# Two projections side by side through the tiles of x, and the place of one constants' transfer, in a hybrid decoder trunk

## The chip, the core and the metric

The kernel runs on one core of a Trainium2 chip. The metric is device time in microseconds (us) of one execution; the time of a kernel is the median of its runs. The core has five engines that run side by side, each through its own queue of instructions in order: TensorE (PE in the profile, its weight loads PEld), VectorE (DVE), ScalarE (ACT), GpSimd (POOL) and SyncE (SP, which here only issues transfers). They wait for one another through semaphores.

## The reference

A decoder trunk of two layers over 512 tokens of 1024 channels, in float32. Layer 0 is the one that matters here: its mixer projects the normed x to 1536 columns, of which 512 go to a causal pooling branch (u) and 2 times 512 to a gated causal convolution of width 31 with a LayerNorm and a swish (a and b); both results are concatenated and projected back.

```python
def pool_conv_mixer(h, w_in, pool_w, pool_scale, dw_w, dw_b, ln_g, ln_b, w_out):
    z = h @ w_in
    u, glu_a, glu_b = jnp.split(z, [POOL_W, POOL_W + CONV_W], axis=-1)
    ...
    ya = jnp.einsum("btgc,gcd->btgd", pooled, pool_w).reshape(b, t, POOL_W) * pool_scale
    gl = glu_a * jax.nn.sigmoid(glu_b)
    cv = causal_dwconv(gl, dw_w) + dw_b
    yb = jax.nn.silu(layernorm(cv, ln_g, ln_b))
    return jnp.concatenate([ya, yb], axis=-1) @ w_out

for l in range(DEPTH):
    h = rmsnorm(x, norm_mix_g[l])
    x = x + (pool_conv_mixer(h, ...) if l % 2 == 0 else mla_attention(h, ...))
    x = x + memory_cross_attention(rmsnorm(x, ...), rmsnorm(mem, ...), ...)
    x = x + conv_ffn(rmsnorm(x, norm_ffn_g[l]), ...)
return rmsnorm(x, final_norm_g)
```

## The kernel before

Activations lie with channels on the 128 partitions and the 512 tokens along the free axis, so x is 8 tiles of 128x512. A product of two float32 numbers is made of three passes: each operand is split into a rounded part (`hh`, `wh`: a cast on ACT) and a rest (`hl`, `wl`: a subtraction on DVE), and `mm3` (L177 to 181) multiplies hi by hi, hi by lo and lo by hi. One output tile of a projection over 8 tiles of x is therefore 24 matmuls ("products" below) of 128x512, and each needs a weight block of 128x1024 that SP loads (`load_w`, L169), ACT casts (L173) and DVE subtracts (L174).

The mixer (L871 to L1092) has these stages.

- **Opening** (L878): the first projection, n = 0, takes tile after tile of x as it lands, with the split of x in `Norm.split` (L286 on ACT, L287 on DVE). Its weights come in two halves of 128x512. Behind it the large constants' transfer `con[:, KD:]` (128 rows of 451 numbers) is issued from ACT's queue.
- **Twelve projections** (L1008): `order` is b, a for each of four convolution tiles, then four u. The norm's rate (`row_rate`, from `nat` tiles that ACT squares, L253) is applied afterwards: `finish` (L993) multiplies a projection's PSUM bank by the rate `rb`, which PE spreads over the partitions (L268, after `RB_K` of 8 tiles of the third projection) and ACT copies. `finish` of an a-tile completes a gated tile, `gl`.
- **Taps**: the convolution is 31 multiply-adds on DVE for each of four tiles (L932, L934), less five of the last tile that PE does with diagonal weights `dg` (L938). The 119 DVE taps are handed out in small portions beside other work: `taps(PACE[0])` for each projection from the point at which a `gl` exists, then `PACE[1]` and `PACE[2]` in the steps of the first memory projection (`memory_kv`, 8 steps and 8 steps), then `PACE[3]` in `filler` (L1058). `PACE` is `(3, 3, 2, 3)`.
- **Filler** (L1058 to L1082): the second memory projection (16 steps, each yields 2), then the pooling half of the output projection (8 outputs, each 12 products, two steps of 1 each, L1061 to L1066). When no tap is left, this loop starts the stages of `normalise` (L952), one at a time with the numbers in `LATE` of steps between them: the mean over channels (a matmul on PE, L962), its subtraction and the squares, the sum (transposes on PE, L241), the Newton steps of a reciprocal root on DVE (L222), its spread (L268, `lb`), the scale and the swish. Stages that the loop did not start run behind it (L1084 to L1088).
- **Last**: the convolution half of the output projection (L1090), 8 outputs of 12 products over the four `yb` tiles.

The order that each engine gets is made by a scheduler from the order of the code and from priorities; weight preparation has a priority of 40 instructions ahead (L172). The lines that decide which portion a loop step gets:

```python
for step in filler():
    if left[0]:
        if step == 2 or left[0] % 2:
            taps(PACE[3])
        ...
    if not left[0] and due <= 0 and stage < len(LATE):
        next(late, None)
```

Weight blocks rotate through three buffers (`wh`, `wl`), raw blocks through four (`wr`), PSUM through eight banks. `early_parts` (L158) is a second set of two buffers, which the FFN uses.

Of the kernel before, what the change touches and what calls it, by code (L numbers as in the profile page):

```python
# [15 lines left out]
ALU = mybir.AluOpType  # L16
# [3 lines left out]
P = 128  # L20
# [3 lines left out]
KD = D // P  # L24
# [33 lines left out]
PE_PACE = 2  # L58
PACE = (3, 3, 2, 3)
MEM1_AT = 10  # L60
RB_K = 6
LATE = (1, 4, 1, 3, 1, 4, 1)
FFN_GROUPS = (4, 4, 4, 4, 6)
PLAIN_PAIRS = 5
# [41 lines left out]
def kernel(ctx: ExitStack, tc: tile.TileContext, a):  # L106
    nc = tc.nc
    vec, act, pe, pool, sp = nc.vector, nc.scalar, nc.tensor, nc.gpsimd, nc.sync
# [10 lines left out]
    def uid(s):  # L119
        count[0] += 1  # L120
        return f"{s}{count[0]}"
# [4 lines left out]
    def bank(name="ps", shape=(P, T)):  # L126
        return pp.tile(list(shape), F32, tag="ps", name=uid(name))
# [4 lines left out]
    def f(t):  # L132
        return t.bitcast(F32)


    con = cp.tile([P, NCOL], F32, tag="con", name="con")
# [11 lines left out]
    def load_raw(src, n):  # L148
        raw = wp.tile([P, WCOLS], F32, tag="wr", name=uid("wr"), bufs=4)
        sp.dma_start(raw[:, :n], src)  # L150
        return raw

    def parts():
        hi = wp.tile([P, WCOLS], F32R, tag="wh", name=uid("wh"), bufs=3)
        lo = wp.tile([P, WCOLS], F32R, tag="wl", name=uid("wl"), bufs=3)
        return hi, lo

    def early_parts():  # L158

        hi = wp.tile([P, WCOLS], F32R, tag="wh1", name=uid("wh1"), bufs=2)  # L160
        lo = wp.tile([P, WCOLS], F32R, tag="wl1", name=uid("wl1"), bufs=2)
        return hi, lo

    def low_by_dma(lo, raw, src):

        act.mul(lo, raw, -1.0)  # L166
        pool.dma_start(lo, src, accum_op=ALU.add)  # L167

    def load_w(src, n):  # L169
        raw = load_raw(src, n)  # L170
        hi, lo = parts()
        with tc.high_priority(offset=AHEAD):  # L172
            act.copy(hi[:, :n], raw[:, :n])  # L173
            vec.tensor_tensor(lo[:, :n], raw[:, :n], f(hi[:, :n]), ALU.subtract)  # L174
        return hi, lo

    def mm3(ps, ah, al, bh, bl, first, last, more=False):  # L177

        pe.matmul(ps, ah, bh, start=first, stop=False, skip_group_check=more)  # L179
        pe.matmul(ps, ah, bl, start=False, stop=False, skip_group_check=more)  # L180
        pe.matmul(ps, al, bh, start=False, stop=last, skip_group_check=more)  # L181

    class Linear:
# [6 lines left out]
        def load(self, k):  # L190
            c = k // KD
            if c not in self.w:
                n = min(KD, self.nk - c * KD) * P
                self.w[c] = load_w(self.src[:, c * KD * P:c * KD * P + n], n)
            return self.w[c]
# [9 lines left out]
    def linear(src, xs):  # L205
        return Linear(src, len(xs)).run(xs, 0, len(xs))
# [664 lines left out]
    def mixer(norm, nxt):  # L871
# [3 lines left out]
        def project(i):  # L875
            return linear(a["pc_in"][i], norm.h)

        def opening(i):  # L878

            ps = bank("lin")  # L880
            half = KD // 2
            for k in range(KD):
                if k % half == 0:
                    hi, lo = load_w(a["pc_in"][i][:, k * P:(k + half) * P], half * P)
                sp.dma_start(x[k], a["xT"][:, k, :])
                norm.split(k)
                c = slice(k % half * P, (k % half + 1) * P)
                mm3(ps, hi[:, c], lo[:, c], *norm.h[k], k == 0, k == KD - 1)
            return ps

        def window(i, t):
# [95 lines left out]
        def taps(n):  # L987
            for _ in range(min(n, left[0])):
                next(conv)

        sig, us, parts = {}, [], []
# [13 lines left out]
        order = [(k, i) for i in range(CT) for k in "ba"] + [("u", i) for i in range(CT)]  # L1005
        base = {"b": 2 * CT, "a": CT, "u": 0}
        wait = []
        for n, (kind, i) in enumerate(order):  # L1008
            if n == 2:
                lin.run(norm.h, 0, RB_K)  # L1010
                rb = norm.wide()
                wait.append((kind, i, lin.run(norm.h, RB_K, KD)))
            else:
                wait.append((kind, i, (project if n else opening)(base[kind] + i)))
            if n == 0:
                act.dma_start(con[:, KD:], a["con"][:, KD:])
            if n == 1:
                lin = Linear(a["pc_in"][base[order[2][0]] + order[2][1]], KD)
                lin.load(0)
                norm.r = row_rate(a["xN"], TB, "rx")  # L1020
            elif n > 1:
                if n == MEM_AT[0]:
                    mem.rate()
                if n == MEM_AT[1]:
                    mem.scale()
                if n == MEM_AT[2]:
                    scaled = [], []
                    for _ in memory_gain(0, mem.raw, *scaled):
                        pass
                while len(wait) > 1:  # L1030
                    finish(*wait.pop(0))
                if gl:
                    taps(PACE[0])
# [417 lines left out]
```

## Time and profile before

| What | Value |
|---|---|
| median of 3 runs | 1383.91 us (1382.83 to 1383.95) |
| the profiled execution, its own time | 1383.12 us |
| its span in the trace | 1381.3 us |
| PE busy | 1352.6 us (98%) |
| DVE busy | 1020.0 us (74%) |
| ACT busy | 748.8 us (54%) |
| the chain that ended last | PE 88%, DVE 8%, ACT 2%, issue 1% of the span |

The time of a run is 1.8 us more than its span: work ahead of and behind the first and the last instruction. In the rows below, "start us, duration us, engine, line, operation, output<-inputs, shape, count" stand in this order, and what ended an idle stretch is in brackets at the end. Matmuls overlap, so the distance from one start to the next says how long a product holds PE, and its duration does not.

### The profile page before, as it was taken

How to read it: one execution, taken by the hardware profiler on the slowest of the kernel's cores; microseconds unless marked ns; L12 is line 12 of the kernel's file. 1: busy time of each engine (PE TensorE's matmuls, PEld its weight loads, DVE VectorE, ACT ScalarE, POOL GpSimd, SP SyncE). 2: the span in 40 equal slices, each digit the busy share in tenths (PEclk: the TensorE clock that was granted, in tenths of full speed). 3: DMA queues.
4: the chain of work that ended last, by engine and by line, in shares of the span. 5: the costliest groups of instructions: out<-in, count | busy, mean ns of one | idle time of the engine just before them, and what ended most of it. 6: DMA issues, size and time to landing. Idle time of an engine off the chain costs nothing.

```text
span 1381.3 us, 20270 instructions
## 1 busy us (share of the span) xinstructions
PE 1352.6 (98%) x7756; PEld 1168.1 (85%) x7756; DVE 1020.0 (74%) x1897; ACT 748.8 (54%) x1264; POOL 52.9 (4%) x71
## 2 busy tenths in 40 slices
PE   8999999999989999999999999999999999999997
PEld 6888978888879999999887776888887899999987
DVE  6999989554787777776869775755549777777765
ACT  6416456445655555554447786644556555555433
POOL 0000000001100000000000000000011000000000
PEclk9999999999999999999999999999999999999999
DMA  9335634118835545553321113321486455555421
GB/s 327 99 104 188 217 104 151 61 38 207 184 91 130 159 124 138 134 137 94 106 81 50 43 47 107 107 77 61 124 188 124 130 132 143 134 136 144 111 73 62
DMA packets 57265, 168.01 MB, mean 122 GB/s; under 512 B 6480, under 2 KB 8144, under 8 KB 57168
## 3 DMA queue, kind: packets, MB, share of 16 engines
q1 hardware_dynamic: 47664, 135.55, 30.6%
q0 software_dynamic: 7776, 28.32, 12.3%
q10 hardware_dynamic: 1728, 2.86, 0.6%
q8 instruction: 60, 0.98, 0.3%
q14 instruction: 37, 0.30, 0.1%
HBM read 162.50 MB, written 4.19 MB: 121 GB/s over the span
## 4 chain that ended last, share of the span: by engine, by line
PE 88%; DVE 8%; ACT 2%; issue 1%; DMA 0%; SPq 0%; DVEq 0%; ACTq 0%
PE lin L179 11%; PE lin L181 11%; PE lin L180 11%; PE xyz L179 8%; PE xyz L180 8%; PE xyz L181 8%; PE down L180 4%; PE down L179 4%; PE down L181 4%; DVE cv L934 3%; PE s L1273 1%; PE mpv L1310 1%; DVE wl L174 1%; PE t L1298 1%; PE vx L180 1%
## 5 line engine op out<-in xcount | busy, mean ns | idle before, releaser
L179 PE MATMUL xyz<-th,wh 128*128 128x256 f32 x816 | 230.8, 284 | 10.6 <-ACT q L737 10.6
L181 PE MATMUL xyz<-th,wl 128*128 128x256 f32 x816 | 231.5, 284 | 0.0
L180 PE MATMUL xyz<-tl,wh 128*128 128x256 f32 x816 | 231.3, 284 | 0.0
L173 ACT CAST wh<-wr 128x1024 fp32r<-128x1024 f32 (+3 forms) x120 | 112.7, 944 | 161.8 <-issue 60.6
L179 PE MATMUL lin<-hh,wh 128*128 128x512 f32 x432 | 171.0, 396 | 5.9 <-ACT hh L286 5.9
L179 PEld LDWEIGHTS xyz<-th,wh 128*128 128x128 f32 x816 | 155.7, 192 | 23.2 <-ACT q L737 14.9
L180 PE MATMUL lin<-hl,wh 128*128 128x512 f32 x432 | 169.7, 393 | 0.0
L181 PE MATMUL lin<-hh,wl 128*128 128x512 f32 x432 | 169.2, 392 | 0.2 <-DVE wl L174 0.2
L180 PEld LDWEIGHTS xyz<-tl,wh 128*128 128x128 f32 x816 | 156.8, 192 | 7.1
L174 DVE TENSOR_TENSOR wl<-wr,wh 128x1024 fp32r<-128x1024 f32 (+3 forms) x120 | 130.1, 1086 | 42.4 <-ACT wh L173 40.9
L181 PEld LDWEIGHTS xyz<-th,wl 128*128 128x128 f32 x816 | 156.7, 192 | 0.0
L565 DVE TENSOR_TENSOR wl<-ws,wh 128x1024 fp32r<-128x1024 f32 x68 | 83.3, 1225 | 61.4 <-ACT wh L564 47.9
L564 ACT CAST wh<-ws 128x1024 fp32r<-128x1024 f32 x68 | 71.3, 1049 | 103.9 <-PE xyz L180 101.3
L179 PE MATMUL down<-fh,dwh 128*128 128x512 f32 x256 | 101.9, 398 | 1.2 <-ACT dwh L218 1.2
L180 PE MATMUL down<-fl,dwh 128*128 128x512 f32 x256 | 102.0, 398 | 0.0
L181 PE MATMUL down<-fh,dwl 128*128 128x512 f32 x256 | 100.5, 393 | 0.5 <-DVE dwl L219 0.5
L179 PEld LDWEIGHTS lin<-hh,wh 128*128 128x128 f32 x432 | 81.6, 189 | 22.3 <-ACT hh L286 6.2
L180 PEld LDWEIGHTS lin<-hl,wh 128*128 128x128 f32 x432 | 81.5, 189 | 18.5 <-DVE hl L287 2.7
L181 PEld LDWEIGHTS lin<-hh,wl 128*128 128x128 f32 x432 | 81.5, 189 | 17.5 <-DVE wl L174 0.6
L167 POOL DMA_DIRECT2D wl<-in_ffn_up x54 | 46.9, 868 | 1058.2 <-ACT wl L166 1058.2
L934 DVE SCALAR_TENSOR_TENSOR cv<-a,con,cv 128x509 f32<-128x509 f32 (+25 forms) x115 | 79.4, 726 | 0.1
L670 ACT ACTIVATE c<-c 128x512 f32<-128x512 f32 x44 | 27.8, 632 | 58.5 <-DVE c L669 58.3
(404 smaller groups left out, 3152.1 us busy)
## 6 DMA issues: line engine op xcount, KB each, us to landing
wr<-in_ffn_up SPq DMA_DIRECT2D x88, 512.0 KB, 4.1
wl<-in_ffn_up POOLq DMA_DIRECT2D x54, 512.0 KB, 5.7
dr<-in_ffn_down SPq DMA_DIRECT2D x64, 256.0 KB, 4.2
wr<-in_xa_wk SPq DMA_DIRECT2D x16, 512.0 KB, 3.5
wr<-in_xa_wv SPq DMA_DIRECT2D x16, 512.0 KB, 4.3
wr<-in_xa_wq SPq DMA_DIRECT2D x16, 512.0 KB, 3.5
wr<-in_xa_wo SPq DMA_DIRECT2D x16, 512.0 KB, 3.5
wr<-in_ffn_down SPq DMA_DIRECT2D x16, 384.0 KB, 3.3
```

The costliest lines, as they stand in the source:

```text
L167: pool.dma_start(lo, src, accum_op=ALU.add)
L173: act.copy(hi[:, :n], raw[:, :n])
L174: vec.tensor_tensor(lo[:, :n], raw[:, :n], f(hi[:, :n]), ALU.subtract)
L179: pe.matmul(ps, ah, bh, start=first, stop=False, skip_group_check=more)
L180: pe.matmul(ps, ah, bl, start=False, stop=False, skip_group_check=more)
L181: pe.matmul(ps, al, bh, start=False, stop=last, skip_group_check=more)
L564: act.copy(hi[:, :n], raw)
L565: vec.tensor_tensor(lo[:, :n], raw, f(hi[:, :n]), ALU.subtract)
L670: act.activation(c, c, AF.Silu)
L934: vec.scalar_tensor_tensor(cv[i][:, s:], gl[i][:, :T - s], w, cv[i][:, s:], ALU.mult, ALU.add)
L1273: pe.matmul(ps[i], q[:, i * P:(i + 1) * P], k[:, :P * (i + 1)], start=True, stop=True)
L1298: pe.transpose(banks[b][:, c:c + P], prob[n][i][:, j * P:(j + 1) * P], ident)
```

## The change

Four things change. The opening now takes two output tiles: b0 and a0 go through the tiles of x together, each with its weights in two halves of 128x512; the second one's split weights lie in the `early_parts` buffers. The large constants' transfer moves from behind the first projection to behind the last split of x, and is held at that place in program order. `RB_K` goes from 6 to 2 and now counts in the fourth projection (n = 3), so `rb` is made there, and `finish` first runs at n = 3 with three projections at once where it ran at n = 2 with two. The third projection is a plain one.

```diff
-RB_K = 6
+RB_K = 2
...
+    pieces = parts, early_parts
...
-        def opening(i):
-
-            ps = bank("lin")
+        def opening(tiles):
+
+            ps = [bank("lin") for _ in tiles]
             half = KD // 2
+            w = {}
+
+            def load(n, k):
+                raw = load_raw(a["pc_in"][tiles[n]][:, k * P:(k + half) * P], half * P)
+                hi, lo = pieces[n]()
+                act.copy(hi[:, :half * P], raw[:, :half * P])
+                vec.tensor_tensor(lo[:, :half * P], raw[:, :half * P], f(hi[:, :half * P]), ALU.subtract)
+                w[n] = hi, lo
+
+            def product(n, k):
+                c = slice(k % half * P, (k % half + 1) * P)
+                mm3(ps[n], w[n][0][:, c], w[n][1][:, c], *norm.h[k], k == 0, k == KD - 1)
+
             for k in range(KD):
                 if k % half == 0:
-                    hi, lo = load_w(a["pc_in"][i][:, k * P:(k + half) * P], half * P)
+                    load(0, k)
                 sp.dma_start(x[k], a["xT"][:, k, :])
                 norm.split(k)
-                c = slice(k % half * P, (k % half + 1) * P)
-                mm3(ps, hi[:, c], lo[:, c], *norm.h[k], k == 0, k == KD - 1)
+                if k % half == 0:
+                    load(1, k)
+                product(0, k)
+                if k % half:
+                    if k % half == 1:
+                        product(1, k - 1)
+                    product(1, k)
+            tc.keep_in_program_order(act.dma_start(con[:, KD:], a["con"][:, KD:]))
             return ps
...
         for n, (kind, i) in enumerate(order):
-            if n == 2:
+            if n == 0:
+                opened = opening([base[kind] + i for kind, i in order[:2]])
+            if n < 2:
+                wait.append((kind, i, opened[n]))
+            elif n == 2:
+                wait.append((kind, i, lin.run(norm.h, 0, KD)))
+            elif n == 3:
+                lin = Linear(a["pc_in"][base[kind] + i], KD)
                 lin.run(norm.h, 0, RB_K)
                 rb = norm.wide()
                 wait.append((kind, i, lin.run(norm.h, RB_K, KD)))
             else:
-                wait.append((kind, i, (project if n else opening)(base[kind] + i)))
-            if n == 0:
-                act.dma_start(con[:, KD:], a["con"][:, KD:])
+                wait.append((kind, i, project(base[kind] + i)))
...
-                while len(wait) > 1:
+                while len(wait) > 1 and n > 2:
                     finish(*wait.pop(0))
                 if gl:
                     taps(PACE[0])
```

Line numbers behind the opening grow by 2 to 26 in the changed kernel. The order that the engines get differs in three places of the mixer.

**ACT, the end of the opening.** `hh` are the splits of x, `wh` weight casts, `dg` the diagonals for PE's taps (they read the large constants), `nat` the squares for the norm's rate. Before:

```order
L944 ACTIVATE dg_736<-ident,con 128x128
L286 ACTIVATE hh_138<-x_77,con 128x512
L944 ACTIVATE dg_739<-ident,con 128x128
L286 ACTIVATE hh_146<-x_78,con 128x512
L944 ACTIVATE dg_769<-ident,con 128x128
L286 ACTIVATE hh_154<-x_79,con 128x512
L944 ACTIVATE dg_772<-ident,con 128x128
L286 ACTIVATE hh_162<-x_80,con 128x512
L173 CAST wh_173<-wr_171 128x1024
```

The same place in the changed kernel:

```order
L288 ACTIVATE hh_196<-x_80,con 128x512
L909 DMA con<-in_con 128x451
L175 CAST wh_210<-wr_208 128x1024
L965 ACTIVATE dg_739<-ident,con 128x128
L175 CAST wh_285<-wr_283 128x1024
L255 ACTIVATE nat_215,rxp_214<-nat_215 128x512
L255 ACTIVATE nat_218,rxp_214<-nat_218 128x512
L965 ACTIVATE dg_742<-ident,con 128x128
L255 ACTIVATE nat_221,rxp_214<-nat_221 128x512
```

The four diagonals moved from between the splits of x to between the weight casts and the squares, behind the transfer of the constants, which ACT now issues after the last split.

**DVE, where the first projections are finished.** `wl_410` and `wl_447` (before) are the weights of n = 5 and n = 6, `wl_413` and `wl_450` in the changed kernel; `b` and `a` are finished tiles, `cv` the taps. Before:

```order
L234 SCALAR_TENSOR_TENSOR rxy_237<-rxt_239,rxy_237 128x4
L174 TENSOR_TENSOR wl_410<-wr_407,wh_409 128x1024
L995 TENSOR_TENSOR b_283<-lin_92,rb_275 128x512
L995 TENSOR_TENSOR a_286<-lin_170,rb_275 128x512
L1000 TENSOR_TENSOR a_286<-a_286,b_283 128x512
L932 TENSOR_SCALAR cv_88<-a_286,con 128x512
L934 SCALAR_TENSOR_TENSOR cv_88<-a_286,con,cv_88 128x511
```

The same place in the changed kernel:

```order
L236 SCALAR_TENSOR_TENSOR rxy_243<-rxt_245,rxy_243 128x4
L176 TENSOR_TENSOR wl_413<-wr_410,wh_412 128x1024
L176 TENSOR_TENSOR wl_450<-wr_447,wh_449 128x1024
L1016 TENSOR_TENSOR b_360<-lin_92,rb_300 128x512
L1016 TENSOR_TENSOR a_363<-lin_93,rb_300 128x512
L1016 TENSOR_TENSOR b_366<-lin_207,rb_300 128x512
L1021 TENSOR_TENSOR a_363<-a_363,b_360 128x512
L1016 TENSOR_TENSOR a_403<-lin_282,rb_300 128x512
L953 TENSOR_SCALAR cv_88<-a_363,con 128x512
```

One more weight block, that of n = 6, now stands ahead of the first finished tile.

**PE, the output projection.** `lin` are outputs of the output projection, their inputs `yah`, `yal` the pooling branch and `ybh`, `ybl` the convolution branch; `mean`, `st` and `rb` are PE's three parts of the convolution's LayerNorm. Before, the mean stands between the first and the second output of the pooling half (`st` and `rb` stand 31 and 50 rows further on, between later outputs):

```order
L179 MATMUL lin_1608<-yah_1019,wh_1611 128x512
L180 MATMUL lin_1608<-yal_1020,wh_1611 128x512
L181 MATMUL lin_1608<-yah_1019,wl_1612 128x512
L962 MATMUL mean_1636<-lacc_1623,om_1627 128x512
L179 MATMUL lin_1638<-yah_928,wh_1641 128x512
L180 MATMUL lin_1638<-yal_929,wh_1641 128x512
```

In the changed kernel the three stand here:

```order
L181 MATMUL lin_1751<-yah_1022,wh_1754 128x512
L182 MATMUL lin_1751<-yal_1023,wh_1754 128x512
L183 MATMUL lin_1751<-yah_1022,wl_1755 128x512
L983 MATMUL mean_1782<-lacc_1776,om_1780 128x512
L243 MATMUL st_1800<-ident,lsq_1784 128x128 x4
L270 MATMUL rb_1824<-ident,lny_1809 128x128 x4
L181 MATMUL lin_1887<-ybh_1839,wh_1890 128x512
L182 MATMUL lin_1887<-ybl_1840,wh_1890 128x512
```

All three moved behind the eighth and last output of the pooling half (`lin_1751`), and follow one another directly, ahead of the first product of the convolution half.

## The prediction

> **What bounds the kernel now.** I read the waits of PE first, since PE is busy 98% of the span: what PE waits for is nearly all that can be won at once.
>
> ```profile
> PE lin L179 <- ACT hh L286: 5.9, 1, 5.9
> PE mean L962 <- DVE lacc L957: 1.5, 1, 1.5
> ```
>
> The columns are the total in us, the times, and the longest. The first is the time to the first product; the second is the only real wait of the mixer, at the mean of its LayerNorm. Next I read PE in order of time in the opening:
>
> ```profile
> 5.85 0.80 PE L179 MATMUL lin<-hh,wh 128*128 128x512 f32 x1 [5.85 <-ACT hh L286]
> ...
> 16.25 0.40 PE L179 MATMUL lin<-hh,wh 128*128 128x512 f32 x1
> ...
> 21.02 0.39 PE L179 MATMUL lin<-hh,wh 128*128 128x512 f32 x1
> ...
> 26.46 0.60 PE L268 MATMUL rb<-ident,rxy 128*128 128x128 f32 x4
> ```
>
> The row at 16.25 is the 4th product of the second projection, the one at 21.02 the first of the third: 21 products in 4.77 us, **0.227 us a product** (24 are 5.44) once all is there. The first two projections, 48 products, took 21.02 - 5.85 = 15.2 us, where 48 at 0.227 are 10.9. So some 4 us are lost in the opening, to the slow first products and to the pace of x.
>
> The end of the mixer, PE first, is the other place that I need:
>
> ```profile
> 177.71 0.39 PE L179 MATMUL lin<-yah,wh 128*128 128x512 f32 x1
> ...
> 182.07 1.10 PE L962 MATMUL mean<-lacc,om 128*128 128x512 f32 x2 [1.47 <-DVE lacc L957]
> ...
> 189.86 0.60 PE L241 MATMUL st<-ident,lsq 128*128 128x128 f32 x4
> ...
> 194.57 0.65 PE L268 MATMUL rb<-ident,lny 128*128 128x128 f32 x4
> ...
> 203.26 0.39 PE L179 MATMUL lin<-ybh,wh 128*128 128x512 f32 x1
> ```
>
> From 177.71 to 203.26 PE does the 96 products of the pooling half, and between them the mean, `st` and `rb`. Between these three, DVE and ACT work for 7 us, 4 us and 8 us, and PE is covered by products all that time. This cover is what the change touches.
>
> **Why the cover goes.** It follows from counting taps, without a time in it. Before, `gl` exists from n = 2, so `PACE[0]` hands out 10 times 3 = 30 taps; the first memory projection 8 times 3 and 8 times 2 = 40; the second 16 times 3 = 48. That leaves 119 - 118 = **1** tap at the first step of the pooling half. One is odd, so `step == 2 or left[0] % 2` holds, the tap is handed out, and `normalise` starts in the loop. In the changed kernel `finish` waits for n = 3, so only 27 are handed out first, and 119 - 27 - 40 - 48 = **4** are left. The steps now yield 1, and 4 is even: none is handed out in 16 steps, `left[0]` never reaches 0, and all stages of `normalise` are emitted behind the loop. The order of the built program agrees: mean, `st` and `rb` stand behind the last pooling product.
>
> **The change part by part.**
>
> *Opening.* PE's clock and the pace of the first products:
>
> ```profile
> 5.85:10.20 4.35, 4.35 (x9) 1.00 1.03 379
> 402.00:406.00 4.00, 4.00 (x17) 0.50 0.30 93
> ```
>
> Nine products started in the first 4.35 us, 0.48 each, though this column grants 1.00 there; the changed kernel has the same x0 first, so I leave these nine as they are. From 10.2 on PE has 39 products left and, with two outputs for each tile of x, always one ready: 39 at 0.227 are 8.9, so the third projection starts at 10.22 + 8.9 + 0.2 for the change of pace = 19.3 instead of 21.02, **1.7 us earlier**. Two more transfers of 256 KB ahead of the last x, and 225 KB of constants fewer, leave the bytes ahead of the last x nearly equal; its last split (12.95 before, see below) may move by a microsecond and still be ahead of PE's need at about 18.
>
> *Constants and rate.* ACT's part of the opening:
>
> ```profile
> 12.95 0.71 ACT L286 ACTIVATE hh<-x,con 128x512 fp32r<-128x512 f32 x1
> ...
> 16.40 0.63 ACT L253 ACTIVATE nat<-nat 128x512 f32<-128x512 f32 x1
> ```
>
> ```profile
> con<-in_con ACTq DMA_DIRECT2D x1, 225.5 KB, 4.0
> ```
>
> ```profile
> 24.94 0.16 DVE L234 SCALAR_TENSOR_TENSOR rxy<-rxt,rxy 128x4 f32<-128x4 f32 x1
> ...
> 28.65 0.68 DVE L995 TENSOR_TENSOR b<-lin,rb 128x512 f32<-128x512 f32 x1
> ```
>
> The first `dg` now waits for the large constants, and queued behind it on ACT are a weight cast and all squares of the rate. Issued at about 12 (12.95 less the four diagonals that are gone) with the 4.0 us to landing of the row above, the constants are there at 16.0; with the diagonal (0.3) and the cast (0.95) the squares start at 17.3, 0.9 late, and three more diagonals between them make 1.8. The rate, 24.94 before, is there at 26.8, `rb` can start at about 27.2. PE would be at `rb` after 31 more products, 19.3 + 7.0 = 26.3. So PE waits 0.9 there, and the lead shrinks from 1.7 to about 0.8. Bounds: no wait (lead 1.7), or the constants 2 us later behind the other transfers (lead -1).
>
> *DVE.* `wl_450` now stands ahead of the first finished tile, and its buffer is free when PE ends n = 3: 27.2 + 0.4 + 17 products = 31.5, plus 2.2 (before, 26.46 to 28.65) is 33.7. DVE starts on taps **5 us later** than at 28.65. What it costs depends on what DVE has to do before each weight block:
>
> ```profile
> 53.41 0.65 DVE cv L934
> 54.06 1.14 DVE wl L174
> ```
>
> At the blocks of the second half of the first memory projection, where PE stands closest behind DVE (below), the changed order has 8 taps and one block fewer ahead: 8 x 0.65 + 1.14 = 6.3 us less work, so the block comes 1.3 us earlier than before. At the third block of the pooling half only the one block is missing, and it comes 5.0 - 1.1 = 3.9 us later, at about 180; PE needs it at 177.71 + 5.4 + 0.2 - 0.8 = 182.5. So I take no new wait on DVE; the margin is 2 us.
>
> ```profile
> 118.12 0.39 PE L179 MATMUL vx<-wh,mh 128*128 128x512 f32 x1
> 118.58 0.50 PE L180 MATMUL vx<-wl,mh 128*128 128x512 f32 x1
> ```
>
> Here PE waited 118.58 - 118.12 - 0.23 = 0.2 us for DVE, which goes. **Lead at the pooling half: 1.0 us**, bounds -1 and 2.
>
> *The end of the mixer.* The pooling half runs through: 177.71 - 1.0 + 96 x 0.227 = 198.5. There PE meets the mean; its input is long there. Then the chain that was covered, with no other work between its links on DVE and ACT:
>
> ```profile
> 21.70 0.17 DVE L256 TENSOR_SCALAR rxq<-rxq 128x4 f32<-128x4 f32 x1
> ...
> 23.69 0.17 DVE L233 TENSOR_TENSOR rxt<-rxt,rxnv 128x4 f32<-128x4 f32 x1
> ```
>
> ```profile
> 183.20 2.48 DVE L966 TENSOR_TENSOR cv<-cv,mean 128x512 f32<-128x512 f32 x4 [0.68 <-PE mean L962]
> 185.60 0.68 DVE L970 TENSOR_TENSOR lsq<-lsq,lq 128x512 f32<-128x512 f32 x1
> ...
> 190.49 0.69 DVE L243 TENSOR_REDUCE ssum<-st 128x4 f32<-128x512 f32 x1 [0.41 <-PE st L241]
> 191.22 0.17 DVE L261 TENSOR_SCALAR lnv<-ssum 128x4 f32<-128x4 f32 x1
> ...
> 195.88 2.50 DVE L977 TENSOR_TENSOR cv<-cv,lb 128x512 f32<-128x512 f32 x4
> ...
> 201.94 0.69 DVE L219 TENSOR_TENSOR ybl<-cv,ybh 128x512 fp32r<-128x512 f32 x1
> ```
>
> ```profile
> 195.26 0.59 ACT L270 COPY lb<-rb 128x512 f32<-128x512 f32 x1 [0.25 <-PE rb L268]
> 195.87 1.28 ACT L978 ACT_TABLE_LOAD   x1
> 197.16 2.94 ACT L978 ACTIVATE cv<-cv,con 128x512 f32<-128x512 f32 x4
> ...
> 200.51 0.62 ACT L218 CAST ybh<-cv 128x512 fp32r<-128x512 f32 x1
> ```
>
> Link by link: mean to its first subtraction 183.20 - 182.07 = 1.1; four subtractions 2.4 and, behind the last of them, the last square 0.6 and the last two sums, 1.3, together 4.3; `st` to the reduction 190.49 - 189.86 = 0.6; the reduction 0.7; the Newton steps as at 21.70 to 23.69 and one more, 2.4; `rb` and the copy 195.26 - 194.57 = 0.7; the copy and the table load 197.16 - 195.26 = 1.9; four swishes 2.9; the cast 0.6. Sum **15.2 us**; with the hops of a few hundredths, and with `st` and `rb` on a slow PE, I take 15.7. In before these links took 201.1 - 182.07 = 19 us, since other work stood between them: that is the other bound of this term.
>
> *PE after the stall.* PE's clock after an idle stretch is shown by the FFN:
>
> ```profile
> 401.69 0.58 PE L179 MATMUL xyz<-th,wh 128*128 128x256 f32 x1 [5.42 <-ACT q L737]
> ...
> 406.76 0.28 PE L181 MATMUL xyz<-th,wl 128*128 128x256 f32 x1
> ```
>
> After 5.4 us of idle the clock is 0.50 (window row above) for about 4.9 us, and products take twice as long. The stall here is three times as long, so the convolution half starts slow: its first 12 products at 0.43, the first two 0.65 apart for the rest of `yb`, take 4.9 us instead of 2.7, 2.2 more. The page "TensorE: Matmul & The Clock Gate" of the Trainium skill, section "What's actually happening", has the half clock after an idle window of about 3.4 us and until a busy window of 3.4 us; the trace agrees on the half clock, but shows 4.9 us of it. With 3.4 us of slow clock the sum would be about 0.7 lower.
>
> *Sum.* The convolution half starts, counted as if at full speed, at 198.5 + 15.7 + 2.2 = 216.4 instead of 203.26: 13.1 us later. What follows it has the same order on PE as before and moves along. Against the profiled execution's own 1383.12 that is **1396.2**; that execution is 0.8 below the median of the runs shown, inside their spread of 1.1.
>
> **The rivals.**
>
> 1. *The stall is there, but cheap.* PE comes back warm (for it: `st` and `rb` touch PE in between; against: the FFN rows) and the lead is whole: 1396.2 - 2.2 - 0.7 = 1393.3. Chance 0.2.
> 2. *The stall is there, and the lead is lost too.* The constants land late, and with them the squares, `rb` and the first tap; the 2 us of margin at the pooling half are used up, and PE waits there as well. For it: DVE's start depends on the same diagonal. 1396.2 + 2 + 1 = 1399. Chance 0.13.
> 3. *The change gains.* The place is the mean's row in PE's queue. If PE could take the mean ahead of the pooling products, the chain would be covered as before, and the opening's lead stays, with the 1.5 us wait for `lacc` gone: 1383.1 - 1.0 - 1.5 = 1380.6. It decides as soon as the mean runs more than about 15 us ahead of the last pooling product. Against it: at 182.07 PE stood for 1.47 us at the mean with ready products behind it; it did not go around. Chance 0.02. The same page's section "Step-by-step: what each phase is for" says that only weight loads are pulled ahead and matmuls stay in program order; by that rule this rival is out, and the wait at 182.07 agrees.
> 4. *It comes to nothing.* Most of the chain is shorter with DVE and ACT free, and the stall is near 4 us: the links above do not allow it. 1385. Chance 0.03.
>
> **How the numbers follow.** The forecast has 0.62 at 1396.2. The range takes in rivals 1 and 2 and the bounds of the lead: 1391.5 to 1399.5. About 0.2% (2.8 us) is what a measurement of this kernel can tell from no change. Slower by more than that are the forecast, rivals 1 and 2: 0.95. Rival 4 gives same, 0.03; rival 3 is 2.5 us, at the edge of faster, 0.02.
>
> **What would show it.** Right: PE's wait for `ybh` or `ybl` at the first convolution product, with those at `st` and `rb` some 12 to 15 us in sum, at about 200 to 214 us, then some 10 products about 0.43 apart; no wait for `lacc`; the third projection's first product at about 19.3; `rb` at about 27 with a short wait. Wrong: no idle PE between the last pooling product and the first convolution product, a first tap before 31, or waits of PE for `wl` between 60 and 180 us.

## The result, and the profile after

The changed kernel takes **1405.7 us** (median of 4 runs, 1404.71 to 1406.32), the kernel before 1383.6 in the same comparison (4 runs, 1382.83 to 1383.95): a ratio of **1.016**, 95% interval [1.0148, 1.0174]. It is 22.1 us slower. The forecast was 12.6 us slower; the time lies above its range. The profiled execution took 1405.8 us, 22.7 above that of before.

First the waits of PE in the changed kernel (in us: the total, the times, the longest); rows that are the same before and after, and rows under 1 us, are left out:

```profile
PE lin L181 <- ACT ybh L220: 5.4, 1, 5.4
PE lin L181 <- ACT hh L288: 5.1, 1, 5.1
PE st L243 <- DVE lsq L991: 5.1, 1, 5.1
PE rb L270 <- DVE rxy L236: 3.7, 1, 3.7
PE rb L270 <- DVE lny L236: 3.2, 1, 3.2
PE rb L270 <- DVE rmy L236: 1.6, 1, 1.6
PE kx L183 <- DVE wl L176: 1.1, 1, 1.1
```

The row for `lacc` is gone, and two groups of rows are new. `st`, `rb` for `lny`, and `ybh` are the chain at the end of the mixer, 13.7 us in sum, as forecast. The second group was not forecast in this size or not at all: 3.7 us at `rb` for the rate of x (`rxy`), 1.6 at the memory's `rb` (`rmy`, the norm's rate of the memory), 1.1 at `kx` (the memory's keys) for a weight block.

PE in order of time, first the opening, then the mixer's end:

```profile
18.92 0.39 PE L181 MATMUL lin<-hh,wh 128*128 128x512 f32 x1
...
29.83 0.67 PE L270 MATMUL rb<-ident,rxy 128*128 128x128 f32 x4 [3.72 <-DVE rxy L236]
30.21 0.72 PE L182 MATMUL lin<-hl,wh 128*128 128x512 f32 x1
...
33.70 0.40 PE L181 MATMUL lin<-hh,wh 128*128 128x512 f32 x1
...
183.74 0.39 PE L181 MATMUL lin<-yah,wh 128*128 128x512 f32 x1
...
205.50 1.02 PE L983 MATMUL mean<-lacc,om 128*128 128x512 f32 x2
211.62 1.11 PE L243 MATMUL st<-ident,lsq 128*128 128x128 f32 x4 [5.11 <-DVE lsq L991]
215.90 1.12 PE L270 MATMUL rb<-ident,lny 128*128 128x128 f32 x4 [3.16 <-DVE lny L236]
222.44 0.79 PE L181 MATMUL lin<-ybh,wh 128*128 128x512 f32 x1 [5.42 <-ACT ybh L220]
...
228.02 0.50 PE L181 MATMUL lin<-ybh,wh 128*128 128x512 f32 x1
```

The third projection begins 2.1 us earlier than before (21.02), the pooling half 6.0 us later (177.71): what the opening won is lost, and 6 us more, between these two rows. The 8 products from 30.21 to 33.70 stand about 0.43 apart, and so do most of the first 12 of the convolution half, 222.44 to 228.02.

What `rb` waited for shows on ACT in order of time:

```profile
12.81 0.36 ACTq L909 DMA_DIRECT2D con<-in_con  x1
...
18.92 0.40 ACT L965 ACTIVATE dg<-ident,con 128x128 f32<-128x128 f32 x1 [3.79 <-DMA con<-in_con]
...
20.17 0.63 ACT L255 ACTIVATE nat<-nat 128x512 f32<-128x512 f32 x1
```

And in the row of the constants' transfer (KB, us from issue to landing):

```profile
con<-in_con ACTq DMA_DIRECT2D x1, 225.5 KB, 6.0
```

In the kernel before, the transfer stands behind the first projection in the code, but the order that ACT got has it at the very start:

```profile
1.19 0.46 ACTq L1016 DMA_DIRECT2D con<-in_con  x1
```

In the changed kernel it is issued at 12.81 and lands 6.0 us later, not 4.0 as before. ACT stands 3.79 us at the first diagonal, with the squares of the rate queued behind it. On DVE the last step of the rate then starts at 29.53 (24.94 before), and the first finished tile is written at 37.97, 9.3 us later than before (28.65):

```profile
29.53 0.15 DVE L236 SCALAR_TENSOR_TENSOR rxy<-rxt,rxy 128x4 f32<-128x4 f32 x1
...
37.97 0.68 DVE L1016 TENSOR_TENSOR b<-lin,rb 128x512 f32<-128x512 f32 x1
```

### The profile page after: what moved, and what is told of

Read it like the earlier page. It is cut to its first block, busy times and chain, and to the rows that moved or that the text cites. A ratio compares the mean times of both kernels' runs of the same rounds, so it can differ in the third digit from the quotient of the medians.

```text
span 1404.0 us, 20272 instructions
## 1 busy us (share of the span) xinstructions
PE 1357.6 (97%) x7756; PEld 1172.5 (84%) x7756; DVE 1020.2 (73%) x1898; ACT 750.0 (53%) x1265; POOL 52.8 (4%) x71
## 3 DMA queue, kind: packets, MB, share of 16 engines
q10 hardware_dynamic: 1728, 2.86, 0.6%
## 4 chain that ended last, share of the span: by engine, by line
PE 85%; DVE 8%; ACT 2%; issue 1%; DMA 1%; SPq 0%; DVEq 0%; ACTq 0%
PE lin L181 11%; PE lin L182 11%; PE lin L183 11%; PE xyz L181 8%; PE xyz L182 8%; PE xyz L183 8%; PE down L182 4%; PE down L181 4%; PE down L183 4%; DVE cv L955 2%; PE s L1299 1%; PE mpv L1336 1%; DVE wl L176 1%; PE t L1324 1%; PE fin L182 1%
## 5 line engine op out<-in xcount | busy, mean ns | idle before, releaser
L182 PEld LDWEIGHTS lin<-hl,wh 128*128 128x128 f32 x432 | 81.9, 190 | 17.3 <-DVE hl L289 1.0
L955 DVE SCALAR_TENSOR_TENSOR cv<-a,con,cv 128x482 f32<-128x482 f32 (+28 forms) x115 | 79.3, 727 | 0.0
```

Of the source, the lines that this page charges most:

```text
L955: vec.scalar_tensor_tensor(cv[i][:, s:], gl[i][:, :T - s], w, cv[i][:, s:], ALU.mult, ALU.add)
```

## The experiments

Each kernel is compared with the kernel before on the same chip; times are medians, and the difference is to the kernel before of that comparison (1383.0 to 1384.0).

### The chain at the end of the mixer

**Handing the taps out on an even number too** (`no_parity`): the changed kernel without the condition.

```diff
-                if step == 2 or left[0] % 2:
-                    taps(PACE[3])
+                taps(PACE[3])
```

> The changed kernel with one condition gone: in the filler loop the remaining taps are handed out at every step, also when an even number is left. Theory A (the LayerNorm's stages were pushed behind the pooling half by four left-over taps): the mean, st and rb stand between pooling products again, the conv half starts about 208 us instead of 225.3, time 1405.7 - 17 = 1388.7 (1387 to 1391). Rival B (the stall stands because DVE ends its taps late anyway, the first of them having started 9 us later than before): PE waits for lacc at the mean instead, 1394 or more.

1389.6 us (+6.6, ratio 1.0049 [1.0035, 1.0064]): 15.5 us of the 22.1 are gone. The mean runs again among the pooling products. PE in order of time in this kernel:

```profile
183.67 0.39 PE L181 MATMUL lin<-yah,wh 128*128 128x512 f32 x1
...
188.83 1.10 PE L983 MATMUL mean<-lacc,om 128*128 128x512 f32 x2
196.94 0.66 PE L243 MATMUL st<-ident,lsq 128*128 128x128 f32 x4 [1.07 <-DVE lsq L991]
202.09 0.65 PE L270 MATMUL rb<-ident,lny 128*128 128x128 f32 x4
208.95 1.02 PE L181 MATMUL lin<-ybh,wh 128*128 128x512 f32 x2
```

The chain is covered but for 1.07 us, and the convolution half starts on a fast PE. Most of what is left, 6.0 of 6.6 us, is there at the first row already: 183.67 instead of 177.71, as in the changed kernel.

**The same without the change's opening** (`before_27`): the kernel before, with the 3 taps of n = 2 left out of that place, so that 4 are left at the pooling half, an even number, as in the changed kernel. Nothing else is touched.

```diff
-                if gl:
+                if gl and n > 2:
                     taps(PACE[0])
```

> The kernel before, with one edit: the third projection hands out no taps, so 27 instead of 30 go to the projections and 4 are left at the pooling half; nothing of the opening is changed. Theory A: the stall appears in full, by the changed kernel's numbers 199.5 (the pooling half run through) + 16.9 (chain) + 2.9 (slow clock) = 219.3 instead of 203.3 for the start of the conv half, 1383.6 + 16 = 1399.6 (1397.5 to 1401). Rival (the late start of DVE and of the rate makes the stall): within 2 us of the kernel before.

1399.5 us (+16.5, ratio 1.0123 [1.0106, 1.014]), as expected. Its waits of PE have the three rows of the changed kernel in the same sizes:

```profile
PE lin L179 <- ACT ybh L218: 5.4, 1, 5.4
PE st L241 <- DVE lsq L970: 5.1, 1, 5.1
PE rb L268 <- DVE lny L234: 3.2, 1, 3.2
```

So three taps handed out at another place cost over 1% by themselves, with no other work added or removed. The step of the prediction on which the forecast loss rested is shown from both sides.

**The slow clock behind the stall** (`warm`): the changed kernel with transposes of the identity between the links of the chain, into a bank that nothing reads, so that PE is kept busy while it waits. In the trace they stand as 44, 24 and 36.

```diff
+        spare = bank("spare")
         for n, _ in enumerate(late):
+            for _ in range((0, 40, 0, 24, 40, 0)[n]):
+                pe.transpose(spare[:, :P], ident, ident)
```

> The changed kernel with PE kept busy in the stall: 44, 24 and 36 transposes of the identity into a spare bank behind the mean, st and rb; their result is not read. Theory A (2.9 us of the stall is PE's slow clock behind the idle stretch, and some tenths of st and rb): the first products of the conv half stand 0.23 to 0.6 apart, not 0.43 throughout, 1405.7 - 3.2 = 1402.5 (1401.8 to 1403.5). Rival (the first products are paced by ybl from DVE, 0.6 for each of four tiles): no gain, 1405.7 within 0.7.

1403.7 us (+20.3, ratio 1.0143 [1.0129, 1.0157]), 2.0 below the changed kernel and 0.2 above the range of theory A. The stage by itself shows more. The columns are the window, its length, PE's busy time with its instructions, and the granted clock. The changed kernel:

```profile
216.00:222.00 6.00, 1.01 (x4) 0.50 0.00 0
222.00:228.00 6.00, 5.56 (x12) 0.50 0.00 0
```

The same windows of this kernel:

```profile
216.00:222.00 6.00, 4.58 (x40) 1.00 0.00 0
222.00:228.00 6.00, 5.41 (x23) 1.00 0.00 0
```

With the clock at 1.00 throughout, twice as many instructions start in the last window. From the mean to `ybh` this run needs 16.0 us instead of 16.9, and its first 12 products 2.9 instead of 5.6: 3.6 us in all. In total only 2.0 arrive. Of the 1.6 us between, 1.1 are there when the mean starts, 206.56 instead of 205.50, and they come from another loss of the clock, at the memory's rate; the rest is open. The wait there and the window around it (its length, PE's busy time, the granted clock), in this kernel:

```profile
53.35 0.66 PE L270 MATMUL rb<-ident,rmy 128*128 128x128 f32 x2 [2.34 <-DVE rmy L236]
53.00:55.00 2.00, 1.65 (x5) 0.58 0.86 289
```

The same place in `no_parity`:

```profile
53.81 0.40 PE L270 MATMUL rb<-ident,rmy 128*128 128x128 f32 x2 [2.86 <-DVE rmy L236]
53.00:55.00 2.00, 1.19 (x7) 1.00 0.90 317
```

A wait of 2.34 us cost the clock in one execution, and a longer one of 2.86 did not in another. In the stall at the end of the mixer the slow clock costs 3.6 us, near the 3.2 that were expected, and it is the smaller part of the stall.

### The constants

**The transfer early again** (`con_early`): the changed kernel, with the constants issued where nothing pins them, so that they go out ahead.

```diff
-            tc.keep_in_program_order(act.dma_start(con[:, KD:], a["con"][:, KD:]))
...
+                act.dma_start(con[:, KD:], a["con"][:, KD:])
```

> The changed kernel with the constants' transfer issued where the scheduler puts it (at the start of ACT's queue), not pinned behind the last split of x. Theory A (the pinned transfer lands at 18.9, holds the first diagonal, and with it the squares of the rate, rb, and all that DVE does with rb): the waits at rb (3.7), at the memory's rate (1.6) and at kx (1.1) go, and the 1.7 of slow clock behind the first, 1405.7 - 8 = 1397.6 (1396.5 to 1399.5). Rival B (two more weight blocks ahead of x and of the rate's input make the rate late): the wait at rb stays at 2 us or more, 1403 or more. The stall at the end of the mixer stays under both.

1400.3 us (+17.3, ratio 1.0128 [1.0113, 1.0143]): 4.8 of the 22.1 us gained, where 8 were expected. The wait for `rxy` is gone (`rb` at 27.08, none ahead of it), and the pooling half starts at 178.07 instead of 183.74. The wait at `kx` stays at 1.1: it does not come from the constants. That is part of what is missing of the 8 us. In this execution PE's slow products behind the stall also last longer, from 216.70 to 223.13.

**Both edits** (`both`): `no_parity` and `con_early` together.

> Both edits at once: no condition on an even number, and the constants' transfer early. If the two losses are separate they add: 1405.7 - 17 - 8 = 1380.7 (1379.5 to 1382.5), 1 to 3 us under the kernel before. Rival: with PE earlier, the mixer is held by DVE's taps, PE waits 2 us or more for lacc at the mean, 1383 to 1386.

1385.7 us (+2.7, ratio 1.0023 [1.0014, 1.0033]): the rival's time, 1383 to 1386, and not the gain; but the rival's wait for `lacc` is not there, so that it was right on the time alone. With the two great losses gone, the changed kernel is still slower than before. The waits of PE in this kernel that the kernel before does not have:

```profile
PE kx L183 <- DVE wl L176: 1.1, 1, 1.1
PE st L243 <- DVE lsq L990: 1.1, 1, 1.1
PE rb L270 <- DVE rmy L236: 1.1, 1, 1.1
```

**The pin alone** (`pin_only`): the kernel before, with its transfer kept in program order.

```diff
-                act.dma_start(con[:, KD:], a["con"][:, KD:])
+                tc.keep_in_program_order(act.dma_start(con[:, KD:], a["con"][:, KD:]))
```

> The kernel before, with the constants' transfer pinned behind the last split of x and nothing else changed. Theory A (the transfer lands at about 18.5, one square of the rate stands ahead of the first diagonal here): rate about 2.5 us later, PE waits some 2 us at rb, no slow clock behind it, 1383.0 + 3 = 1386 (1385 to 1388). Rival (the pin costs only together with the two outputs): within 0.7 of the kernel before.

1384.4 us (+1.0, ratio 1.0009 [1.0, 1.0019]): between the two theories. The wait at `rb` came as theory A had it, with no slow clock, but the time is below its 1385 to 1388. The landing is late as in the changed kernel, but the order on ACT is not the same. ACT in order of time in this kernel:

```profile
11.31 0.36 ACTq L1016 DMA_DIRECT2D con<-in_con  x1
...
14.91 0.63 ACT L253 ACTIVATE nat<-nat 128x512 f32<-128x512 f32 x1
17.64 0.40 ACT L944 ACTIVATE dg<-ident,con 128x128 f32<-128x128 f32 x1 [2.02 <-DMA con<-in_con]
```

Its transfer of the constants:

```profile
con<-in_con ACTq DMA_DIRECT2D x1, 225.5 KB, 6.3
```

Issued 1.5 us earlier and with a square ahead of the first diagonal, the same pin gives a rate at 26.69 instead of 29.53, and PE waits 1.98 us, after which its products go on 0.23 apart. Of the 2.8 us by which the rate is earlier, 1.3 are the earlier landing, 0.9 a weight cast that stands behind the first diagonal in the changed kernel and ahead of it here, and 0.6 the square. The pin's price is not a number of its own: it depends on what stands behind the diagonal.

**The diagonals out of the way** (`dg_late`): the changed kernel with its pin, and with the diagonals kept in program order too, so that they stand behind the squares.

```diff
-                act.activation(dg, ident, AF.Identity, scale=col("conv_dw_w", (CONV_K - 1 - s) * CT + i))
+                tc.keep_in_program_order(
+                    act.activation(dg, ident, AF.Identity, scale=col("conv_dw_w", (CONV_K - 1 - s) * CT + i)))
```

> The changed kernel with one edit: the diagonals for PE's taps keep their place in program order, behind the projections, so that the squares of the rate no longer stand behind a diagonal that waits for the constants; the transfer stays pinned. Theory A (the queue behind the diagonal is what the pinned transfer costs): no wait or under 1 us at rb, the time of the run with the early transfer, 1400.3 (1399 to 1401.5). Rival (the transfer itself, in the middle of the rate's input, delays it): the wait at rb stays above 2 us, 1403 or more.

1402.0 us (+18.6, ratio 1.0134 [1.0121, 1.0148]), 3.7 below the changed kernel and 1.7 above `con_early`, just outside what was expected. `rb` has no wait for `rxy` (28.73), though the transfer takes 5.8 us here. The last step of the rate starts at 26.50 instead of 29.53: so it was the diagonal in front of the squares that made the rate late. That no wait at all is left owes something to chance, since PE came to `rb` only at 28.73, and in the changed kernel it stood there from 26.1. Where the 1.7 us are that stay is not settled: in its profiled execution the third projection began at 21.70, against 20.05 in that of `con_early`, and the rate was 1.8 us later than there (24.68).

### The later rate and finish

**The opening alone** (`side_only`): the changed kernel's opening with two outputs, the transfer early, and `rb` and the first finish at n = 2 as before.

```diff
-RB_K = 2
+RB_K = 6
...
-            tc.keep_in_program_order(act.dma_start(con[:, KD:], a["con"][:, KD:]))
...
+                act.dma_start(con[:, KD:], a["con"][:, KD:])
...
             elif n == 2:
-                wait.append((kind, i, lin.run(norm.h, 0, KD)))
-            elif n == 3:
-                lin = Linear(a["pc_in"][base[kind] + i], KD)
                 lin.run(norm.h, 0, RB_K)
...
-                while len(wait) > 1 and n > 2:
+                while len(wait) > 1:
...
```

> The changed kernel's opening with two outputs side by side, and nothing else of the change: the constants' transfer early, rb in the third projection with 6 of 8 tiles, finish and taps from the third projection on, as in the kernel before. Theory A (the opening itself wins what PE saves there; the waits at the memory's rate and at kx that are left with both edits come from the later rb and finish): no wait at kx, none at the memory's rate, rb up to 1 us earlier, 1383.0 - 1.0 = 1382.0 (1380.8 to 1383.0). Rival (DVE, full from 30 to 175 us, sets the mixer's end whatever PE does): PE waits longer for lacc at the mean, within 0.3 of the kernel before.

1382.8 us (11 runs) against 1383.35 (21 runs): ratio 0.9995 [0.9986, 1.0003], no difference. In its trace `rb` runs at 25.65, 0.8 earlier than before, the pooling half starts at 176.86 (0.85 earlier) and the convolution half at 202.38 (0.9 earlier). The lead is there and survives, but it is 0.9 us, too little to be told from nothing by the times.

**The later rate alone** (`rb_late`): the kernel before with only that part of the change, and with the taps handed out on even numbers too.

```diff
-RB_K = 6
+RB_K = 2
...
             if n == 2:
+                wait.append((kind, i, lin.run(norm.h, 0, KD)))
+            elif n == 3:
+                lin = Linear(a["pc_in"][base[kind] + i], KD)
                 lin.run(norm.h, 0, RB_K)
...
-                while len(wait) > 1:
+                while len(wait) > 1 and n > 2:
...
-                if step == 2 or left[0] % 2:
-                    taps(PACE[3])
+                taps(PACE[3])
```

> The kernel before with only the later rate: `rb` and the first finish behind the fourth projection, and no condition on an even number, so that the pooling half's LayerNorm stays covered. The opening is that of the kernel before. Theory A (the later `rb` and finish cause the waits at `kx` and `rmy` and the 2 us that are left in the kernel with both edits): waits of PE of about 1.1 us at `kx` and about 1 at `rmy`, and 1385.6 us (1384.5 to 1387). Rival (these waits come from the opening with two outputs): no such waits, and within 0.7 of the kernel before (1382.7 to 1384).

1386.2 us (+2.2, ratio 1.0017 [1.0008, 1.0027]): theory A. The waits of PE that the kernel before does not have:

```profile
PE kx L181 <- DVE wl L174: 1.1, 1, 1.1
PE st L241 <- DVE lsq L970: 1.1, 1, 1.1
PE rb L268 <- DVE rmy L234: 0.5, 1, 0.5
```

The last step of the memory's rate on DVE, in this kernel:

```profile
49.72 0.15 DVE L234 SCALAR_TENSOR_TENSOR rmy<-rmt,rmy 128x2 f32<-128x2 f32 x1
```

The same step in the kernel before, with PE's use of it, from all engines in order of time:

```profile
48.01 0.15 DVE L234 SCALAR_TENSOR_TENSOR rmy<-rmt,rmy 128x2 f32<-128x2 f32 x1
...
48.69 0.38 PE L268 MATMUL rb<-ident,rmy 128*128 128x128 f32 x2
```

Before, the memory's rate ended at 48.16 and PE used it at 48.69: 0.5 us of margin. Here, with the first finish after 35 us instead of 28.65, the rate ends 1.7 us later, and the margin is gone. Of the 1.7 us, 0.6 are there at the rate of x already (25.57 instead of 24.94: this execution's opening was later), and 1.1 come behind it. The three rows of `both` name the same three places.

### A PE that is fast from the first product

The opening begins at 0.43 or more from product to product, though the granted clock in the profile reads 1.00. Three kernels put 22 transposes of the identity ahead of the first product, into a bank that nothing reads:

```diff
+    spare = bank("spare")
+    for _ in range(22):
+        pe.transpose(spare[:, :P], ident, ident)
```

**With the opening alone** (`prewarm`):

> The changed opening alone, with the constants issued early and `rb` where it was before, and 22 transposes of the identity ahead of the first product, into a bank that nothing reads. Theory A (the opening loses 1 to 2 us to a PE that starts slow): the first products stand 0.23 apart where x is there, the third projection starts at 18.5 to 19 instead of 20.2 us, and the time is 1381.5 us (1380.5 to 1382.5). Rival (the opening goes at the pace of x and its splits, or the mixer is held by DVE, not by PE's lead): the third projection starts no earlier than 19.8, or it does and the time is within 0.5 of 1382.8.

1386.8 us (+2.85, ratio 1.0019 [1.001, 1.0028]): the first half of theory A (an earlier third projection) and the contrary of the second (a shorter time). PE in order of time in this kernel:

```profile
18.78 0.39 PE L184 MATMUL lin<-hh,wh 128*128 128x512 f32 x1
...
25.48 1.11 PE L273 MATMUL rb<-ident,rxy 128*128 128x128 f32 x4 [2.46 <-DVE rxy L239]
```

The window around that wait (its length, PE's busy time, the granted clock 0.66):

```profile
24.00:29.00 5.00, 3.52 (x11) 0.66 0.65 195
```

The end of the rate on DVE:

```profile
25.27 0.15 DVE L239 SCALAR_TENSOR_TENSOR rxy<-rxt,rxy 128x4 f32<-128x4 f32 x1
```

The third projection begins 1.4 us earlier than in `side_only`, as expected, but the rate is no earlier (25.27 against 24.61). PE waits 2.46 us for it, falls to its slow clock, and the pooling half starts 4.0 us later than in `side_only` (180.88). The transposes also moved the order: `rb` now stands behind 18 products of the third projection, not 24.

**With `rb` behind all 24** (`prewarm8`):

```diff
-RB_K = 6
+RB_K = KD
```

> The opening with two outputs and the 22 transposes ahead of it, the constants issued early, and `rb` behind the whole third projection instead of six of its eight tiles. Theory A (in the run with transposes PE came 2.5 us too early for the rate, fell to its slow clock and lost its lead by that alone): the third projection starts at about 18.8, PE comes to `rb` at about 24.4 and waits about 1.0 for `rxy` at 25.4, its clock stays at 1.00 behind it, the pooling half starts at 175.5 to 176 instead of 177.7, and the time is 1381.5 us (1380.8 to 1382.5). Rival (the mixer's front goes at DVE's pace, whatever PE's lead): waits of PE at `kx`, `rmy` or `lacc` take the lead back, 1383 to 1385.

1384.1 us (+1.0, ratio 1.0009 [1.0, 1.0017]): the rival. `rb` waits 1.07 us, the clock holds, and the lead is lost further on, at `rmy` (1.54 us); the pooling half starts at 178.04.

**Before, with the transposes alone** (`before_warm`):

> The kernel before with only the 22 transposes ahead of the first product. Theory A (the first products are slow because PE starts on its slow clock, and the rate at 25.1 leaves room for 1.3 us): the first products stand about 0.23 apart where x is there, `rb` comes at about 25.2 to 25.5 instead of 26.5, with a wait of less than 0.5, and the time is 1382.7 us (1382 to 1383.5), 0.5 to 1.5 below the kernel before. Rival (one output for each tile of x leaves PE waiting for the splits whatever its clock): the third projection starts within 0.4 of 21.0, and the time is that of before within 0.5.

1385.7 us (+2.6, ratio 1.0018 [1.0009, 1.0027]), which neither theory expected. `rb` runs at 25.57, 0.9 earlier than before, behind 18 products and a wait of 0.7; then a wait of 0.7 at `kx` appears, and the pooling half starts at 179.54. How much of this is the order that the transposes moved and how much DVE's pace, these runs do not separate. None of the kernels is measurably faster than the one before.

## Why the prediction fell short, point by point

Four kernels take the 22 us apart, one part after the other, each by its difference to the kernel before: `side_only` -0.5; `both`, which adds the later rate and finish, +2.7; `con_early`, which adds the even number of taps, +17.3; the changed kernel, which adds the pinned transfer, +22.1. The parts are -0.5, **3.2**, **14.6** and **4.8**, each good to 1 to 3 us by the intervals of the ratios. Taken in another order they differ by about as much: the pinned transfer costs 3.9 from `both` to `no_parity`, and the even number of taps 15.5 from `no_parity` to the changed kernel.

- *Why the cover goes* was right: 4 taps left, none handed out, the LayerNorm behind the loop. `before_27` shows it alone and `no_parity` takes it away. Its price in the sum was 199.5 (the pooling half run through without a lead) + 15.7 + 2.2 - 203.26 = 14.1; the two runs that differ by it alone with the transfer early give 14.6.
- *The chain* was taken at 15.7 and measures 222.44 - 205.50 = 16.9: `st` and `rb` take 1.1 us each on the slow clock instead of 0.6; on the fast clock of `warm` it is 16.0, so that 0.9 of the 1.2 missed are the clock. *PE after the stall* was taken at 2.2 and measures 5.58 - 12 x 0.227 = 2.9. Most of that is in the sum itself: twelve distances, one of 0.65 and eleven of 0.43, are 5.4 us and not the 4.9 that it took. Both terms together are 1.9 too small.
- *Opening* came out near the forecast: the third projection begins at 18.92 in this execution (19.3 forecast). That is in part luck, since this start is not one number. With the same opening it is 18.92, 21.03 (`warm`), 21.70 and 22.30 in the four kernels with the pinned transfer, and 20.05 to 20.51 in the three with the early one, as the second tile of x is split and as PE leaves its slow products earlier or later. `no_parity`, with the latest of them, starts its pooling half at 183.67, the changed kernel, with the earliest, at 183.74: the early PE waited 3.7 us at `rb` and 1.6 at `rmy`, the late one 0.6 and 2.9. With the rate this late, the opening's pace does not matter: `rb` ran at 29.83, 30.11 and, in `warm`, 30.18.
- *Constants and rate* is **the step that failed**. It took 4.0 us to landing from the one row there was, and that transfer had been issued early. It gave a bound of 2 us more, and the 2 us more came: 6.0, and 5.8 to 6.3 in all five kernels with the pin, against 4.0 to 4.5 in the nine without. Issued at 12.81 instead of 12, it landed at 18.8 instead of 16.0, and the squares began at 20.17 instead of 17.3. The last step of the rate started at 29.53 instead of 26.8, and PE waited 3.7 instead of 0.9.
- *What a longer wait brings* was left out of that step: after 3.7 us PE was on its slow clock, and 8 products cost 30.21 to 33.70, 3.5 us instead of 1.8. The row behind the 5.4 us wait of the FFN stood in the prediction, but was used for the mixer's end alone.
- *"I take no new wait on DVE; the margin is 2 us"* failed too. The first finish was forecast at 33.7 and came at 37.97. And the place with the smallest margin, the memory's rate at 48.69 with 0.5 us, was not among those that I looked at, nor was `kx`, where PE waits 1.1 us for a weight block at 141.33. A wait for `wl` between 60 and 180 us was one of the signs that I had named for being wrong, and it came. `rb_late` shows 2.2 us for it with the first finish at 35.2, near the forecast's 33.7: even with the constants in time the term was not nothing.

From the trace, the pooling half starts at 183.74, where the forecast's lead of 1.0 gave 176.7. It is late by 2.6 (`rb` at 29.83, forecast 27.2) + 1.7 (the slow products) + 1.6 (`rmy`) + 1.1 (`kx`) = 7.0; with the 1.9 of the chain and the clock that is 8.9 of the 9.5 us by which the forecast missed. Rival 2 named this mechanism, constants late and DVE with them, and priced it at 3 us; but the wait that it expected at the pooling half did not come, and the waits came at the memory's rate and at `kx`.

The page "TensorE: Matmul & The Clock Gate" of the Trainium skill, section "What's actually happening", has the half clock after an idle window of about 3.4 us, which is free-running. The wait of 3.72 at `rb` agrees, and waits of 1.98 and 1.07 left the clock alone. The waits of 2.34 in `warm` (0.58 in its window) and 2.46 in `prewarm` (0.66) cost it, though they are shorter than the page's 3.4 us, and the longer wait of 2.86 in `no_parity` left it at 1.00. So the length of a wait alone does not decide it here; that a free-running window would spare one wait and not another is a reading that no run here tests.

## What to carry to other kernels

Where a change moves a step that hands out work in portions, count what is left over at every later place that asks for it: here a remainder of 4 instead of 1 cost 14.6 us. Before an engine is given a lead, find what it must meet next (here the rate of x, then the memory's rate), and read the margin there; a lead that ends in a wait is worth nothing, and a wait of 2.3 us or more can cost the clock as well (2.34, 2.46 and 3.72 us did, 2.86 did not). A transfer's time from a row holds for its place: moved behind others, take the bound and not the row.

## What the runs showed of the hardware

- The same transfer of 225.5 KB on ACT's queue took 4.0 to 4.5 us from issue to landing when it was issued early, and 5.8 to 6.3 when it was issued at 11 to 13 us, behind the transfers of x. What in the DMA engines makes the difference was not tried.
- PE's slow products lasted from 25.5 to 28.5 us after the 2.46 us wait of `prewarm`, from 29.83 to 33.70 after 3.72 us, from 222.44 to 228.02 after the chain, and from 216.70 to 223.13 after the same chain in `con_early`. In the opening they come with a granted clock that reads 1.00; the transposes ahead of them removed them (products 0.23 apart from 9.25 us on, and before that waits of 0.3 to 0.6 us for the split of x), so the distance of 0.43 is PE's and not that of x.
- This one is the scheduler's and not the chip's: 22 instructions at the very start, whose results no other instruction reads, changed the order in which `rb` stands among the products of the third projection, 20 us later. An edit that looks local is to be compared in the built order before it is priced.
